# Issuing the weight loads of the output projection and the FFN from GpSimd

## The chip, the cores and the metric

The kernel runs on one core of a Trainium2 chip. The metric is device time in microseconds for one execution; the time before is the median of three runs, and a profile of one execution is read beside it.

## The reference

One transformer block on 2,048 tokens of width 1,024, in float32. The core of it:

```python
h = rms_norm(x, g_attn) * (1 + sc_a) + sh_a
aq, ak, av, bq, bk, bv, iq, ik, iw = split(h @ w_in)
o_a = diff_attention(aq, ak, av)           # 4 heads, dense, difference of two softmaxes
o_b = dsa_attention(bq, bk, bv, iq, ik, iw)  # 8 heads over the 256 keys that an indexer picks
x = x + gt_a * (concat(o_a, o_b) @ w_out)
h = rms_norm(x, g_ffn) * (1 + sc_f) + sh_f
u = causal_dwconv(h @ w_up)                # 3 taps along the tokens, 2 * 2816 columns
x = x + gt_f * ((silu(u_gate) * u_val) @ w_down)
```

## The kernel before

Each float32 factor of a product is held as two fp16 parts, high and low, and `acc3` (lines 399 to 404) adds three matmuls per block of 128: high by high, high by low, low by high. The kernel has two phases. In the first, about the first 600 us and parts of the next 150, the weights are split into their two parts and written to DRAM (`wo_s`, `wu_s`, `wd_s`), and the projections by `w_in` are made. The second phase takes the 16 blocks of 128 tokens in six runs, `RUNS = [(0, 2), (2, 2), (4, 4), (8, 4), (12, 2), (14, 2)]` (first block, number of blocks). Each run has its selection (I), its dense attention (A), its sparse attention (B, C) and its output projection and FFN (F).

`ffn` (line 1257) does F. `out_proj` multiplies the mixed heads by `w_out` (16 tiles `wo` for four blocks, 8 for two). Then, for each of two halves of the hidden width, come 22 chunks of `w_up` of 128 columns (tiles `wu`, a gate chunk and a value chunk by turns), the convolution and the gate, and then the product by `w_down` (tiles `wd`, two output halves of six tiles each for every two blocks). All three kinds of tile share one ring of three buffers of 512 KB, 4 KB in each partition (`tag="wu"`, `BUFS["wu"]` is 3; the sixth `wd` of a half is 256 KB). So a load can start when the matmuls that read the third tile before it are done, and there are 64 + 264 + 192 = 520 such loads.

The convolution of a chunk is spread over three engines. ScalarE copies the product out of PSUM to `ut` (line 1274) and makes the third tap `ua` (line 1276), VectorE adds the second tap (line 1277), and GpSimd makes the first tap `u0` (line 1279), adds it (line 1280), and moves the two last columns from and to `halo` (lines 1273 and 1281). GpSimd also multiplies value by gate, once per two chunks (line 1287). Its work for the attention is small: a power for a norm (line 992), the mask added to a bias (line 1152) and the power of the second norm (line 1241).

The order of the work comes from generators that yield their cost: `timeline` (line 1314) always advances the part that is due next, so that F of a run goes beside the attention of the next one (`fpos`, `FK`). The F of the last run, blocks 14 and 15, has no attention left beside it. A scheduler then fixes each engine's program, in order, by its own clock; every engine and every issuing queue works through its list without overtaking. All transfers are issued by SyncE (SP below): the 520 weight loads, 480 DMA transposes of the attention weights (`pT`, line 922), and the keys, values, queries, masks and rows of x.

```python
wu = Z.tile([P, 2, KD, P], F16, name="wu", tag="wu", bufs=BUFS["wu"])
nc.sync.dma_start(wu, wu_s[cc // 4][:, cc % 4])
ps = mm_ps(w=n)
acc3(ps, lambda hl, k: wu[:, hl, k], lambda hl, k: hT[:, hl, k, :n], KD)
```

Of the kernel before, what the change touches and what calls it, by code (L numbers as in the profile page):

```python
# [13 lines left out]
F16 = mybir.dt.float16  # L14
# [6 lines left out]
DRAM = bass.MemoryType.DRAM  # L21

P = 128
# [17 lines left out]
# natural groups of columns of w_in: (name, [(first column, width)], kept width)  # L41
# [10 lines left out]
# share of the next run that a run's FFN is spread over  # L52
FK = [1, 1, 1, 1.2, 1.2, 1]
# from where to where in the second phase: first projections, others, selection, dense part, sparse part of two blocks
E0 = dict(M=(0, .1), N=(.1, 1), I=(0, .5), A=(0, .4), B=(.4, .7), C=(.7, 1))
# work of the preparation of the weights
RESTN = 4 + 13 * 9 + 37 + 11 * 5
SMALL = 6
SHORT = 8                # the block below which VectorE counts one block of two for all bits
ORDER = [4, 5, 3, 0, 1, 2]  # L60
NE = 4                   # tiles projected in the first phase
BUFS = dict(r2k=7, sq=2, wst=4, k4=4, big=4, ring=10, nb=5, q=4, qi=2, ki=2, hl=3, pT=4, f2k=8, g=12, wu=3, mask=2)
ATT0 = dict(big=6, ring=4, nb=5, q=4, ki=1, hl=3, pT=3)
# rates of that preparation, beside the projections and beside the first tiles
R_REST = 0.75
R_FIRST = 0.4
# runs of blocks of 128 tokens that the attention and the FFN take together
RUNS = [(0, 2), (2, 2), (4, 4), (8, 4), (12, 2), (14, 2)]
# from where to where among the runs their selection is made
# [3 lines left out]
def bucket_starts():  # L73
    """First distance of each of the buckets 17..31."""
    n = np.arange(1, 512, dtype=np.float32)
    large = 16 + (np.log(n / np.float32(16)) / np.float32(math.log(8.0)) * np.float32(16)).astype(np.int32)
    large = np.minimum(large, 31)
    return [int(n[np.argmax((large >= b) & (n >= 16))]) for b in range(17, 32)]
# [3 lines left out]
def block_kernel(ctx: ExitStack, tc, x, c, w_ada, b_ada, g_attn, w_in, q_norm_a, k_norm_a, q_norm_b, k_norm_b,  # L82
# [16 lines left out]
    # ---------------------------------------------------------------- constants  # L99
# [13 lines left out]
    def pow2_floor(out_, in_):  # L113
        """out_ = the largest power of two not above in_ > 0."""
        V.tensor_scalar(out_.bitcast(I32), in_.bitcast(I32), EXPM, None, op0=ALU.bitwise_and)

    def pow2_inv(out_, in_, e):
        """out_ = 2^e / in_ for in_ a power of two."""
        V.tensor_scalar(out_.bitcast(I32), in_.bitcast(I32), -1.0, float((254 + e) << 23), op0=ALU.mult, op1=ALU.add)

    def all_max(pool, out_, in_):
        """out_ = the largest magnitude of the column in_, in all partitions."""
# [6 lines left out]
    def woven(*gens):  # L129
        """The generators in step, each (generator, its work) at its own rate."""  # L130
# [20 lines left out]
    def pipeline(units):  # L151
        """Each unit is a list of generators, its stages; a stage runs in step with the next stage of the unit before."""
# [22 lines left out]
    # rows of 128 features to columns  # L175
# [35 lines left out]
    # ---------------------------------------------------------------- modulation  # L211
# [6 lines left out]
    def set_anchor(bi):  # L218
        """Work that is held is issued behind the newest anchor of its engine."""
# [8 lines left out]
    def pace(bi):  # L228
        """While pacing, side work keeps its place among the main work."""
# [19 lines left out]
    def ada(pool, g):  # L249
        """A part of the modulation, summed on VectorE: as columns, or (2, 5) as a row in all partitions."""  # L250
# [29 lines left out]
    def h_scale(pool, name, gT, g0):  # L280
        """Columns of the gain and shift of h, times a power of two that keeps |h|_2 < 2^14, and that power."""
# [18 lines left out]
    # ---------------------------------------------------------------- weights  # L300
    def w_load(pool, src):
        """The rows of 128 x nk of src, in two tiles."""
# [7 lines left out]
    def scale_of(mx, s, inv):  # L310
        """s = the power of two that brings the root of mx under 2^15, inv = 1 / s."""
# [7 lines left out]
    def prep(pool, tiles, dst, w, inv, s_out=None, n2_out=None, done=None, held=False, gain=None):  # L319
        """dst(i, 0 / 1) = the fp16 high and low parts of tiles[i] (times the row gain) * s, s a power of two that keeps  # L320
        the norm of every column (n2_out: the largest, squared), or else of all of it, under 2^15; inv gets 1 / s."""
# [54 lines left out]
    # ---------------------------------------------------------------- h = norm(x) * g + s, transposed, in two parts  # L376
    def rms_rows(xt, n, xn, junk):
        """xn = the n rows of 1024 of xt, normalised."""
# [8 lines left out]
    def h_chunk(pool, xn, k, gp, sp, hT, c0, tag, bufs):  # L387
        """hT[:, 0 / 1, k, c0...] from the normalised rows, 128 each."""
# [10 lines left out]
    def acc3(ps, a, b, nk, k0=0, first=True, last=True):  # L399
        """ps = sum over k of (a0 + a1)[k]^T (b0 + b1)[k] without the product of the low parts."""  # L400
# [5 lines left out]
    def split(hi, lo, src, scale):  # L406
        """hi + lo = src * scale."""
# [3 lines left out]
    # ---------------------------------------------------------------- scalars of the attention parts  # L411
    VS = 2.0 ** -14          # products of h and w_in to fp16
    QS = 2.0 ** 12           # normalised queries to fp16
    PB = 14                  # weights of the sparse part to fp16: times 2^PB
# [3 lines left out]
    def gain(pool, name, qg, kg):  # L418
        """Column of q gain * k gain / 8 (twice), times 2^m below 2^12, and 2^-(12 + m)."""
# [17 lines left out]
    # ---------------------------------------------------------------- projections  # L437
    ka_s = [dram.tile([P, 4, 4, 256], F16, name=f"ka_s{t}") for t in range(NT)]    # head, block, k of 2
    va_s = [dram.tile([P, 4, 4, 256], F16, name=f"va_s{t}") for t in range(NT)]    # head, block, v in 2 parts
    kb_s = [dram.tile([P, 2, 4, 256], F16, name=f"kb_s{t}") for t in range(NT)]    # group, block, k in 2 parts  # L440
    vb_s = [dram.tile([P, 2, 4, 128], F16, name=f"vb_s{t}") for t in range(NT)]    # group, block, v in 2 parts
# [20 lines left out]
    def w_in_first(pool, g, wg, tiles):  # L462
        """Parts of a group of w_in to SBUF and to DRAM."""
# [1016 lines left out]
```

## Time and profile before

| what | value |
|---|---|
| time, median of 3 runs (range) | 3296.61 us (3294.74 to 3297.13) |
| span of the profiled execution | 3288.9 us |
| TensorE matmuls (PE), share of the span | 86% |
| VectorE (DVE) | 78% |
| ScalarE (ACT) | 61% |
| GpSimd (POOL) | 37% |
| mean granted TensorE clock | 0.951 of full |
| mean DMA rate | 214 GB/s |

The profiled execution has no time of its own beside its span, which runs from its first to its last instruction; the runs' median is 7.7 us longer. In the profile PE stands for matmuls, PEld for weight loads into TensorE, and SPq for SyncE's queue, which issues transfers and does nothing else. An instruction that issues a transfer from SP is not counted as busy time.

### The profile page before, as it was taken

The page shows a single profiled execution, that of the slowest core. Times are in us where ns is not written, and L with a number is a line of the kernel's source. Part 1 is how long each engine was busy: PE and PEld are TensorE (multiplying, and loading weights), DVE is VectorE, ACT ScalarE, POOL GpSimd, SP SyncE. Part 2 cuts the span into 40 slices and gives each one's busy share as a digit, 9 for nine tenths or more (in the row PEclk, how much of TensorE's full clock was granted, in tenths as well). Part 3 has the DMA queues.
Part 4 walks back from the last instruction along what each step waited for, and adds up shares of the span by engine and source line. Part 5 has one row for each costly group of instructions (what it writes and reads, how often), then busy time and mean ns, then how long its engine had stood idle before and what let it go on. Part 6 is the DMA issues. An engine that isn't in the chain of part 4 may idle for free.

```text
span 3288.9 us, 54138 instructions
## 1 busy us (share of the span) xinstructions
PE 2831.8 (86%) x17571; PEld 1621.2 (49%) x17571; DVE 2573.9 (78%) x6915; ACT 2008.5 (61%) x3773; POOL 1214.3 (37%) x1493
## 2 busy tenths in 40 slices
PE   5879997986889889877998999789889898788899
PEld 2334544442756566533444444444444445556466
DVE  8856889886988999977998788796788977967222
ACT  3757755573755775777456975568746678556122
POOL 2100354220645255501750571006325502835155
PEclk9889998998999899988999999999999999999999
DMA  8699975427687778996458779974786697799776
GB/s 339 184 322 307 357 274 172 148 65 226 189 229 229 203 216 207 254 247 165 123 133 241 184 181 247 268 199 117 207 214 156 156 278 210 192 261 229 215 218 199
DMA packets 747268, 704.07 MB, mean 214 GB/s; under 512 B 480494, under 2 KB 589286, under 8 KB 745704
## 3 DMA queue, kind: packets, MB, share of 16 engines
q1 hardware_dynamic: 746984, 700.62, 76.2%
q8 instruction: 137, 2.24, 0.3%
q14 instruction: 147, 1.20, 0.1%
HBM read 480.88 MB, written 114.20 MB: 181 GB/s over the span
## 4 chain that ended last, share of the span: by engine, by line
PE 32%; DVE 29%; DMA 15%; ACT 10%; issue 10%; POOL 3%; SPq 1%; DVEq 0%; ACTq 0%; POOLq 0%
PE mm L402 8%; PE mm L403 8%; PE mm L404 8%; DMA pT<-hl 7%; ACT cjunk L1081 4%; DVE cjunk L1065 4%; DVE hl L409 3%; DMA wd<-wd_s 3%; DMA xt<-in_x_dram 2%; DVE sc L1043 2%; DMA wu<-wu_s 1%; DVE big L906 1%; DVE ua L1277 1%; DVE big L903 1%; DVE big L973 1%
## 5 line engine op out<-in xcount | busy, mean ns | idle before, releaser
L402 PE MATMUL mm<-h2T,wu 128*128 128x256 f16 (+1 forms) x2112 | 655.9, 311 | 33.8 <-ACT ua L1276 17.4
L404 PE MATMUL mm<-h2T,wu 128*128 128x256 f16 (+1 forms) x2112 | 656.3, 311 | 0.0
L403 PE MATMUL mm<-h2T,wu 128*128 128x256 f16 (+1 forms) x2112 | 655.8, 311 | 0.0
L1081 ACT ACTIVATE cjunk<-sc,sel 128x512 bf16<-128x512 f32 (+10 forms) x281 | 395.8, 1409 | 155.9 <-DVE cjunk L1065 118.7
L1279 POOL TENSOR_SCALAR u<-ut,cws 128x256 f32<-128x256 f32 (+1 forms) x264 | 343.3, 1301 | 343.1 <-ACT ut L1274 295.9
L402 PE MATMUL mm<-wd,gT 128*128 128x512 f16 x704 | 272.5, 387 | 52.8 <-DMA wd<-wd_s 34.8
L1280 POOL TENSOR_TENSOR ua<-ua,u 128x256 f32<-128x256 f32 (+1 forms) x264 | 279.9, 1061 | 60.4 <-DVE ua L1277 49.2
L403 PE MATMUL mm<-wd,gT 128*128 128x512 f16 x704 | 272.3, 387 | 0.0
L404 PE MATMUL mm<-wd,gT 128*128 128x512 f16 x704 | 271.8, 386 | 0.0
L402 PEld LDWEIGHTS <-wu 128*128 128x128 f16 x2112 | 208.8, 99 | 123.4 <-DMA wu<-wu_s 20.9
L403 PEld LDWEIGHTS <-wu 128*128 128x128 f16 x2112 | 208.4, 99 | 122.9 <-issue 25.6
L409 DVE SCALAR_TENSOR_TENSOR hl<-big,hl 128x512 f16<-128x512 f32 (+3 forms) x320 | 207.3, 663 | 72.5 <-ACT hl L408 71.7
L404 PEld LDWEIGHTS <-wu 128*128 128x128 f16 x2112 | 208.1, 99 | 103.6 <-issue 3.5
L408 ACT ACTIVATE hl<-big 128x512 f16<-128x512 f32 (+3 forms) x320 | 172.4, 562 | 140.0 <-DMA pT<-hl 135.4
L402 PE MATMUL mm<-wg,hT 128*128 128x512 f16 (+1 forms) x640 | 243.5, 381 | 16.5 <-DVE kn L487 8.4
L403 PE MATMUL mm<-wg,hT 128*128 128x512 f16 (+1 forms) x640 | 242.9, 380 | 3.0 <-DVE wg L371 3.0
L1277 DVE SCALAR_TENSOR_TENSOR ua<-ut,cws,ua 128x256 f32<-128x256 f32 (+1 forms) x264 | 161.1, 610 | 104.4 <-ACT ua L1276 97.3
L404 PE MATMUL mm<-wg,hT 128*128 128x512 f16 (+1 forms) x640 | 235.3, 377 | 2.2 <-DVE hT L396 2.2
L1043 DVE SCALAR_TENSOR_TENSOR sc<-relu,iw_all,sc 128x512 f32<-128x512 f32 (+3 forms) x266 | 220.3, 828 | 17.7 <-ACT relu L1042 14.5
L481 POOL TENSOR_TENSOR hn_r<-hn_t,mhalf 128x8 f32<-128x8 f32 (+1 forms) x64 | 96.1, 1504 | 371.0 <-DVE hn_t L479 254.6
L992 POOL TENSOR_TENSOR a_ss<-a_ss,mhalf 128x1 f32<-128x1 f32 x64 | 44.2, 690 | 506.9 <-DVE a_ss L991 344.2
L1042 ACT ACTIVATE relu<-si 128x512 f32<-128x512 f32 (+3 forms) x266 | 139.8, 540 | 122.1 <-PE si L1035 75.4
(338 smaller groups left out, 7349.7 us busy)
## 6 DMA issues: line engine op xcount, KB each, us to landing
wu<-wu_s SPq DMA_DIRECT2D x264, 512.0 KB, 4.2
wd<-wd_s SPq DMA_DIRECT2D x160, 512.0 KB, 4.8
wo<-wo_s SPq DMA_DIRECT2D x64, 512.0 KB, 5.0
wst<-in_w_ada_dram SPq DMA_DIRECT2D x22, 1024.0 KB, 12.8
wst<-in_w_up_dram SPq DMA_DIRECT2D x22, 1024.0 KB, 10.5
wu_s<-wp SPq DMA_DIRECT2D x22, 1024.0 KB, 5.8
xd<-x_s SPq DMA_DIRECT2D x64, 256.0 KB, 5.0
ka<-ka_s SPq DMA_DIRECT2D x60, 256.0 KB, 4.6
```

Of the source, the lines that this page charges most:

```text
L402: PE.matmul(ps, a(0, k), b(0, k), start=(first and k == k0), stop=False)
L403: PE.matmul(ps, a(0, k), b(1, k), start=False, stop=False)
L404: PE.matmul(ps, a(1, k), b(0, k), start=False, stop=(last and k == k0 + nk - 1))
L408: S.activation(hi, src, AF.Copy, scale=scale)
L409: V.scalar_tensor_tensor(lo, src, scale, hi, op0=ALU.mult, op1=ALU.subtract)
L1042: S.activation(r, ps, AF.Relu)
L1043: V.scalar_tensor_tensor(sc_[:, c0:c1], r, w, sc_[:, c0:c1], op0=ALU.mult, op1=ALU.add)
L1065: V.tensor_scalar(junk[:, :ns[j]], src[j][:, :ns[j]], C[:, j:j + 1].bitcast(F32), None, op0=op, op1=ALU.add, accum_out=cnt[:, j:j + 1])
L1081: S.activation(junk[:, :ns[j]], scs[j][:, :ns[j]], AF.Sign, bias=C[:, j:j + 1].bitcast(F32), accum_out=cnt[:, j:j + 1])
L1277: V.scalar_tensor_tensor(a, ut[:, 1:n + 1], cws[:, 1, cc:cc + 1], a, op0=ALU.mult, op1=ALU.add)
L1279: G.tensor_scalar(u0, ut[:, 0:n], cws[:, 0, cc:cc + 1], None, op0=ALU.mult)
L1280: G.tensor_tensor(a, a, u0, op=ALU.add)
```

## The change

The three kinds of weight load of the second phase are issued by GpSimd and no longer by SyncE; everything else stays. (The rest of the difference removes comments.)

```diff
@@ out_proj
                     wo = Z.tile([P, 2, 2, 512], F16, name="wo", tag="wu", bufs=BUFS["wu"])
-                    nc.sync.dma_start(wo, wo_s[:, half, k0:k0 + 2])
+                    nc.gpsimd.dma_start(wo, wo_s[:, half, k0:k0 + 2])
@@ ffn
                     wu = Z.tile([P, 2, KD, P], F16, name="wu", tag="wu", bufs=BUFS["wu"])
-                    nc.sync.dma_start(wu, wu_s[cc // 4][:, cc % 4])
+                    nc.gpsimd.dma_start(wu, wu_s[cc // 4][:, cc % 4])
@@ ffn
                         wd = Z.tile([P, 2, 2, 512], F16, name="wd", tag="wu", bufs=BUFS["wu"])
-                        nc.sync.dma_start(wd[:, :k1 - k0], wd_s[half][:, 11 * hf_ + k0:11 * hf_ + k1])
+                        nc.gpsimd.dma_start(wd[:, :k1 - k0], wd_s[half][:, 11 * hf_ + k0:11 * hf_ + k1])
```

The scheduler makes new programs for all engines from this. First, GpSimd's program late in the chunks of `w_up` of the last run, for one pair of chunks (gate and value; the numbers count tiles in the order of the source, names in brackets are semaphores waited for). Before:

```order
L1279 TENSOR_SCALAR u0_36775<-ut_36769,cws_169 128x256 [waits Activation_49]
L1281 COPY halo_174<-ut_36769 128x2
L1273 COPY ut_36806<-halo_174 128x2
L1280 TENSOR_TENSOR ua_36772<-ua_36772,u0_36775 128x256 [waits DVE_49,Pool_49]
L1279 TENSOR_SCALAR u0_36812<-ut_36806,cws_169 128x256 [waits Activation_49,Pool_49]
L1281 COPY halo_174<-ut_36806 128x2
L1273 COPY ut_36850<-halo_174 128x2 [waits DVE_49]
L1280 TENSOR_TENSOR ua_36809<-ua_36809,u0_36812 128x256 [waits DVE_49,Pool_49]
L1287 TENSOR_TENSOR ua_36772<-ua_36772,ua_36809 128x256 [waits DVE_49,Pool_49]
```

The same stretch after the change:

```order
L1269 DMA wu_36698<-wu_s9_153 128x2048 [waits DMASW4_49,PE_49]
L1280 TENSOR_TENSOR ua_36529<-ua_36529,u0_36532 128x256 [waits DVE_49,Pool_49]
L1279 TENSOR_SCALAR u0_36569<-ut_36563,cws_169 128x256 [waits Activation_49,Pool_49]
L1281 COPY halo_174<-ut_36563 128x2
L1269 DMA wu_36742<-wu_s4_148 128x2048 [waits DMASW5_49,PE_49]
L1273 COPY ut_36607<-halo_174 128x2 [waits Pool_49]
L1280 TENSOR_TENSOR ua_36566<-ua_36566,u0_36569 128x256 [waits DVE_49,Pool_49]
L1279 TENSOR_SCALAR u0_36613<-ut_36607,cws_169 128x256 [waits Activation_49,Pool_49]
L1281 COPY halo_174<-ut_36607 128x2
L1273 COPY ut_36644<-halo_174 128x2 [waits DVE_49]
L1287 TENSOR_TENSOR ua_36529<-ua_36529,ua_36566 128x256 [waits Pool_49]
```

The pair keeps its nine operations and gets two loads among them. A load waits for TensorE to be done with the third tile before its own, and the additions of older chunks stand behind it.

Second, GpSimd's program early in the second phase, around the power of one head's norm in the dense attention (`a_ss_11709`, line 992). Before, it stands behind the operations of a chunk of `w_up`:

```order
L1279 TENSOR_SCALAR u0_11231<-ut_11225,cws_169 128x256 [waits Activation_49,Pool_49]
L1281 COPY halo_174<-ut_11225 128x2
L1280 TENSOR_TENSOR ua_11228<-ua_11228,u0_11231 128x256 [waits DVE_49,Pool_49]
L1287 TENSOR_TENSOR ua_11162<-ua_11162,ua_11228 128x256 [waits DVE_49,Pool_49]
L992 TENSOR_TENSOR a_ss_11709<-a_ss_11709,mhalf_70 128x1 [waits DVE_49]
```

After the change:

```order
L1302 DMA wd_9828<-wd_s1_156 128x2048 [waits DMASW4_49,PE_49]
L1302 DMA wd_9855<-wd_s1_156 128x2048 [waits DMASW5_49,PE_49]
L1302 DMA wd_9901<-wd_s1_156 128x1024 [waits DMASW6_49,PE_49]
L1269 DMA wu_9913<-wu_s2_146 128x2048 [waits DMASW7_49,PE_49]
L1269 DMA wu_9979<-wu_s8_152 128x2048 [waits DMASW0_49,PE_49]
L1269 DMA wu_10042<-wu_s3_147 128x2048 [waits DMASW1_49,PE_49]
L992 TENSOR_TENSOR a_ss_11709<-a_ss_11709,mhalf_70 128x1 [waits DVE_49]
L1269 DMA wu_10110<-wu_s8_152 128x2048 [waits DMASW2_49,PE_49]
```

The same power now stands behind loads, each of which waits for TensorE, and beside earlier chunks of the FFN than before (those with numbers near 9,900, where it was 11,225): the scheduler has set the FFN of the first runs later against the attention.

## Rows read from the trace of the kernel before

**Rows 1.** The page: busy time by engine, and the chain that ended last.

```profile
PE 2831.8 (86%) x17571; PEld 1621.2 (49%) x17571; DVE 2573.9 (78%) x6915; ACT 2008.5 (61%) x3773; POOL 1214.3 (37%) x1493
...
PE 32%; DVE 29%; DMA 15%; ACT 10%; issue 10%; POOL 3%; SPq 1%; DVEq 0%; ACTq 0%; POOLq 0%
PE mm L402 8%; PE mm L403 8%; PE mm L404 8%; DMA pT<-hl 7%; ACT cjunk L1081 4%; DVE cjunk L1065 4%; DVE hl L409 3%; DMA wd<-wd_s 3%; DMA xt<-in_x_dram 2%; DVE sc L1043 2%; DMA wu<-wu_s 1%; DVE big L906 1%; DVE ua L1277 1%; DVE big L903 1%; DVE big L973 1%
```

**Rows 2.** Busy time by stretch: from:to and length, PE, PEld, DVE, ACT, POOL, clock, DMA.

```profile
833.00:909.00 76.00, 68.08 (x609) 57.44 (x609) 71.94 (x250) 56.69 (x146) 56.99 (x103) 1.00 0.73 204
952.00:1028.00 76.00, 71.19 (x623) 58.80 (x624) 67.27 (x145) 43.84 (x106) 62.85 (x91) 1.00 0.73 209
1125.00:1207.00 82.00, 76.90 (x671) 63.14 (x670) 78.86 (x264) 63.90 (x148) 58.13 (x97) 0.99 0.72 200
1252.00:1360.00 108.00, 97.44 (x869) 74.47 (x867) 104.43 (x297) 76.94 (x193) 76.79 (x112) 0.98 0.92 222
1808.00:1960.00 152.00, 147.78 (x937) 75.43 (x935) 122.98 (x338) 133.87 (x229) 96.24 (x106) 0.99 0.80 182
...
3104.00:3162.00 58.00, 58.00 (x524) 51.62 (x524) 19.65 (x46) 26.02 (x63) 48.48 (x92) 0.98 0.60 184
3195.00:3254.00 59.00, 57.95 (x527) 51.22 (x527) 19.00 (x43) 25.57 (x62) 48.87 (x94) 1.00 0.69 208
```

**Rows 3.** Timeline of POOL, one pair of chunks of the last run: start, us, operation.

```profile
3116.13 0.92 POOL L1279 TENSOR_SCALAR u<-ut,cws 128x256 f32<-128x256 f32 x1 [0.41 <-ACT ut L1274]
3117.00 0.37 POOL L1281 COPY halo<-ut 128x2 f32<-128x2 f32 x1
3117.31 0.18 POOL L1273 COPY ut<-halo 128x2 f32<-128x2 f32 x1
3117.45 0.72 POOL L1280 TENSOR_TENSOR ua<-ua,u 128x256 f32<-128x256 f32 x1
3118.26 0.72 POOL L1287 TENSOR_TENSOR ua<-ua 128x256 f32<-128x256 f32 x1
3118.96 0.92 POOL L1279 TENSOR_SCALAR u<-ut,cws 128x256 f32<-128x256 f32 x1
3119.83 0.32 POOL L1281 COPY halo<-ut 128x2 f32<-128x2 f32 x1
3120.09 0.18 POOL L1273 COPY ut<-halo 128x2 f32<-128x2 f32 x1
3120.23 0.72 POOL L1280 TENSOR_TENSOR ua<-ua,u 128x256 f32<-128x256 f32 x1
3121.37 0.93 POOL L1279 TENSOR_SCALAR u<-ut,cws 128x256 f32<-128x256 f32 x1 [0.42 <-ACT ut L1274]
```

**Rows 4.** Two issuing lines of SP: ns shortest/median/longest, first and last start.

```profile
L1269 SPq DMA_DIRECT2D wu<-wu_s x264: 319/324/1482, 807.8 to 3246.5; - x132
...
L922 SPq DMA_TRANSPOSE pT<-hl x480: 1167/1239/4354, 592.2 to 3045.3; - x160
```

**Rows 5.** Who waited for whom: us in total, times, longest.

```profile
POOL a_ss L992 <- DVE a_ss L991: 344.2, 34, 73.1
...
PE mm L402 <- DMA wd<-wd_s: 34.8, 31, 6.2
...
PE mm L402 <- DMA wo<-wo_s: 30.3, 15, 10.4
...
PE mm L402 <- DMA wu<-wu_s: 14.3, 12, 2.9
```

**Rows 6.** The same for SP's queue, the two longest on weight loads.

```profile
SPq L1269 <- PE mm L404: 301.5, 115, 12.3
...
SPq L1302 <- PE mm L404: 154.8, 82, 9.0
```

**Rows 7.** Loads of the last run, 3100 to 3289 us: count, KB, median us to landing.

```profile
wu<-wu_s SPq DMA_DIRECT2D x41, 512.0 KB, 4.1
wd<-wd_s SPq DMA_DIRECT2D x20, 512.0 KB, 4.0
```

## The prediction

> **What bounds the kernel now.** I read the page first. TensorE is busy 86% and VectorE 78% of the span, and the chain that ended last changes between TensorE (32%), VectorE (29%) and transfers (15%) [rows 1]: no one engine sets the time throughout. GpSimd (POOL) is busy 37% [rows 1], which looks like room for 520 more instructions. That mean is misleading, so I read the busy times by stretch next. Each stretch shown is one half of an FFN's 22 chunks of `w_up`. In the four early ones (runs of two blocks, with attention beside them) POOL is busy 57.0 of 76, 62.9 of 76, 58.1 of 82 and 76.8 of 108 us; beside the attention of a longer run, with four blocks in the FFN, 96.2 of 152 us [rows 2]. In the last run, where no attention is left, it is busy 48.5 of 58 and 48.9 of 59 us while TensorE is busy without a gap, 58.0 of 58 [rows 2]. So TensorE bounds that stretch and POOL is close behind it.
>
> The timeline of POOL there shows how close. A pair of chunks takes 3121.37 - 3116.13 = 5.24 us, the time of 48 matmuls, and POOL waits in it once, 0.42 us [rows 3]. Its own work is 4.82 us a pair, 92% of it. Eleven such pairs make a half, so 22 pairs stand in the tail. That is where I look for the cost; SP's queue is where I look for the gain.
>
> **The change part by part.** It takes 520 issues from SP and gives POOL the same 520. The bytes and the three buffers stay. The pieces of the order show that the change does this, and where the new instructions stand.
>
> *What an issue costs POOL* is the number on which all rests, and the trace has none: POOL issues nothing before. From below the nearest row is POOL's shortest operation, the copy of two columns, 0.18 us [rows 3]; from above SP's issue of a transpose, 1.24 us median, where a plain issue holds SP 0.32 us [rows 4]. I take 1.0 us. A load of 512 KB is 128 rows of 4 KB, read on one side and written on the other, so 256 entries of a list; POOL's operation on 256 elements per partition takes 0.92 us [rows 3] and the longer of SP's two issues 1.24 us, and I put the list between those. This is a choice, and both ends stay for the range. The Trainium skill (DMA: Bandwidth & Descriptors, "Anatomy of one DMA — SWDGE (gpsimd) path") speaks against it: it calls descriptor generation small and says most of a transfer's fixed cost is its completion, off the engine. By that page the first term below would shrink towards 0; no run here shows it yet.
>
> *The tail's 44 chunks.* A pair on POOL becomes 4.82 + 2 x 1.0 = 6.82 us against TensorE's 5.24, so POOL takes over as the bound: 22 x (6.82 - 5.24) = +34.8 us. With 0.18 us the pair is 5.18, still under 5.24: 0. With 1.24 it is 7.30: +45.3 us. The cover that hid POOL's work was TensorE's matmuls, and 0.42 us a pair is all that was left of it.
>
> *The early stretches of two blocks.* With 22 us each, POOL's demand is 79.0 of 76, 84.9 of 76, 80.1 of 82 and 98.8 of 108 us. The excess is 3.0 + 8.9 = 11.9 us if POOL never waited; at 98% and more it will wait, so I take +15. Some of this comes back, since VectorE is at 71.9 of 76 and 104.4 of 108 us there [rows 2] and attention can use what the FFN leaves. Ends: 0 (0.18 us) and 8.3 + 14.2 + 3.4 = +25.9 (1.24 us). In the runs of four blocks 96.2 + 22 = 118.2 of 152 us fits: 0.
>
> *What queues behind a load on POOL.* A load waits on POOL for TensorE, and what stands behind waits too. The convolution's operations need TensorE's later chunks anyway, so for them it is nearly free. The attention's powers are not tied to the FFN; in the second piece of the order one stands behind three `wd` and three `wu` loads, each released by the end of one tile, 5.24 / 2 = 2.62 us. VectorE waits for that power. Before, POOL mostly stood ready for it: 344.2 us in 34 waits [rows 5], so the power had no slack on POOL's side. I take +8 us for all 64 powers and the mask additions. Ends: 0, and +40 (in each of the 10 `w_down` parts beside attention about 1.5 tiles of 2.62 us).
>
> *Landing.* In the tail a load lands 4.1 (`wu`) or 4.0 us (`wd`) after its issue [rows 7], and with three buffers a tile's round is 2.62 + 4.0 us, a third of which is 2.21. An issue of 1.0 in place of 0.32 us makes it 2.43, still under 2.62: 0, at most +3.
>
> *What SP gains.* Its queue loses 520 x 0.32 = 168 us of issuing, and the waits for TensorE at the head of its queue, 301.5 + 154.8 us for `wu` and `wd` [rows 6], during which nothing behind could start. Little of it lies on the path: SP's queue is 1% of the chain [rows 1], and transposes hold SP 1.24 us each with or without loads between them. What it can give is bounded by TensorE's waits for loads, 34.8 + 30.3 + 14.3 = 79.4 us [rows 5]; about half of these are loads that stood behind other transfers in SP's queue, so -40 at best. But POOL will now make loads late too. I take -10; ends -40 and 0.
>
> *Sum:* 34.8 + 15 + 8 + 0 - 10 = +47.8 us. The profiled execution spans 3288.9 us, the median is 3296.6; I add the change to the median: 3344.4 us, say **3344 us**. All low ends together give 3257, all high ends 3297 + 45 + 26 + 40 + 3 = 3411.
>
> **The rivals.** *Faster: a light issue.* If an issue holds POOL no more than (5.24 - 4.82) / 2 = 0.21 us, TensorE stays the bound of the tail, and what is left is SP's relief: transposes no longer stand behind loads that wait for a buffer, and loads no longer behind transposes. `pT` is 7% of the chain [rows 1], and TensorE's waits for loads are 79.4 us. I give it -30: 3267 us. For it: SP's plain issue is 0.32 us, not far off. Against it: POOL's shortest operation of all is 0.18 us, and a list for 128 rows is more work than copying two columns.
>
> *No change.* An issue somewhere near 0.4 us costs the tail 22 x (5.62 - 5.24) = 8.4 us, the early stretches next to nothing (62.9 + 8.8 of 76), and the gain at SP pays it back: 3297 us. The Trainium skill (DMA: Bandwidth & Descriptors, "Issuing engines are not separate DMA queues") says about this: which engine issues only saves that engine's time, usually small beside the transfer, as all transfers share the same DMA engines. By that rule the time stays within a few us of 3297; the 1% of SP's queue in the chain agrees with its half about SP, and it does not count what else the new issuer has to do.
>
> *Much slower: loads held behind attention.* POOL's list is in order, so a load behind a power waits until VectorE has that power's operand. POOL stood 34 times for this, 10.1 us a time and up to 73.1 us [rows 5]; nothing hung on it. TensorE has two tiles in hand, 5.24 us. Where a wait outlasts those, TensorE stops, and with it the attention's own matmuls in its list. If all 34 waits kept loads behind them, 34 x (10.1 - 5.24) = 165 us; with half of them about 80 us come on top of my sum: 3425 us. For it: the second piece of the order has a load right behind a power. Against it: the scheduler places loads and powers by its clock, and early ones are set apart.
>
> **How the numbers follow.** My case has a chance of 0.64, with 3303 to 3400 as its own range; the light issue 0.14, no change 0.10, loads behind attention 0.12. A measurement can tell 0.2%, 6.6 us, from no change, so from 3290 to 3303 is "same". Faster: 0.14 and a little of "no change", 0.16. Same: most of the rest of that case and the lowest end of mine, 0.08. Slower: 0.76. The range 3284 to 3412 leaves out most of the light issue (0.12) and two thirds of the last rival (0.08); its top is the sum of the high ends.
>
> **What would show it.** In the new profile the 41 loads of `w_up` that fall into the tail should stand among POOL's operations with about 1.0 us each; a pair there should take about 6.8 us where it took 5.24, POOL should have no idle time in it, and TensorE should wait 1.6 us a pair, its busy time in a half near 58 of 75 us. The stretch of the tail should grow by about 35 of the 48 us. The `w_down` parts of the tail should keep their length, and SP's queue should show its transposes starting earlier. I am wrong about the mechanism if the tail keeps its length, and about its size if an issue takes under 0.5 us or the early runs change by more than the tail. TensorE's waits for `wd` and `wo` beyond 79 us in all, or long waits of loads behind powers, would speak for the last rival.

## The result, and the profile after

The changed kernel takes 3465.32 us (median of 4 runs, 3458.48 to 3469.54), the kernel before 3295.68 us beside it (4 runs, 3287.26 to 3297.13). The ratio is 1.0521, 95% interval 1.0497 to 1.0545: 170 us slower, where 48 were forecast. The direction is right; the size lies 53 us above the top of the range. Where single profiles are compared below, the changed kernel's spans 3467.8 us.

The page of the changed kernel, its busy times, queues and chain (compare [rows 1]):

```profile
PE 2901.6 (84%) x17571; PEld 1643.7 (47%) x17571; DVE 2651.3 (76%) x6915; ACT 2015.1 (58%) x3773; POOL 1477.0 (43%) x2013
...
q1 hardware_dynamic: 672104, 436.35, 48.8%
q0 software_dynamic: 72832, 264.27, 25.5%
...
PE 30%; DVE 27%; DMA 20%; issue 10%; ACT 8%; POOL 4%; SPq 1%; DVEq 0%; ACTq 0%; POOLq 0%
DMA pT<-hl 13%; PE mm L402 7%; PE mm L403 7%; PE mm L404 7%; ACT cjunk L1081 3%; DVE cjunk L1065 3%; DVE hl L409 3%; DMA wd<-wd_s 2%; DMA xt<-in_x_dram 2%; DVE big L906 1%; DVE ua L1277 1%; DVE big L903 1%; POOL ua L1280 1%; DMA wo<-wo_s 1%; DVE big L908 1%
```

The 264 MB of the loads now go through a queue of their own (q0). What grew in the chain is the transposes `pT`, from 7% of 3289 us to 13% of 3468, about 220 us more; no other entry shown grew by more than a point. Those transposes were not moved.

Busy times by stretch, the same columns as in [rows 2]: the four halves of early runs, then the two halves of the last run.

```profile
834.00:950.00 116.00, 86.89 (x701) 68.08 (x698) 105.54 (x364) 79.64 (x203) 76.47 (x133) 0.88 0.69 172
997.00:1077.00 80.00, 77.11 (x624) 60.87 (x623) 73.97 (x130) 46.81 (x106) 71.65 (x115) 0.99 0.64 185
1177.00:1273.00 96.00, 81.07 (x679) 65.37 (x679) 94.39 (x266) 60.66 (x143) 79.50 (x122) 0.95 0.67 172
1323.00:1417.00 94.00, 84.16 (x777) 67.61 (x777) 85.88 (x245) 62.69 (x150) 70.90 (x123) 0.98 0.91 217
3258.00:3324.00 66.00, 61.21 (x528) 52.28 (x528) 35.44 (x45) 25.07 (x63) 57.91 (x107) 0.97 0.54 162
3361.50:3427.50 66.00, 59.71 (x528) 51.15 (x529) 33.67 (x40) 24.23 (x61) 58.26 (x108) 1.00 0.60 186
```

A half of the tail takes 66 us where it took 59. The early halves hold other shares of attention than before (364 VectorE operations in the first, where there were 250), so their lengths can't be compared one by one. Therefore I compare three points in time: the first matmul of the third run's output projection, that of the last run's, and the last matmul of all. In the profiled executions these are 1414.4, 3067.9 and 3285.2 us before and 1474.2, 3224.3 and 3464.1 after. So the 179 us between the two profiles fall into three parts:

| part | growth |
|---|---|
| early: up to the third run's output projection | +59.8 us |
| middle: from there to the last run's | +96.5 us |
| tail: the last run's output projection and FFN, no attention beside it | +22.6 us |

Not all of the growth is waiting. TensorE's matmuls, the same 17571, are busy 2901.6 us where it was 2831.8 (the page above and [rows 1]), at a mean granted clock of 0.933 where it was 0.951. Of these 70 us, 37 lie in the middle part and 8 in the tail. The runs below whose middle grows by 90 us or more show it too (granted clock 0.940 in e4, 0.937 in e9, 0.934 in e7, 0.939 in e14). No run separates the lower clock from the waits, so a loss below is both together.

A pair of chunks on POOL in the tail (compare [rows 3]):

```profile
3289.86 1.10 POOL L1279 TENSOR_SCALAR u<-ut,cws 128x256 f32<-128x256 f32 x1
3290.92 0.17 POOL L1281 COPY halo<-ut 128x2 f32<-128x2 f32 x1
3291.04 0.17 POOL L1273 COPY ut<-halo 128x2 f32<-128x2 f32 x1
3291.18 0.71 POOL L1287 TENSOR_TENSOR ua<-ua 128x256 f32<-128x256 f32 x1
3291.85 0.59 POOL L1269 DMA_DIRECT2D wu<-wu_s  x1
3292.46 0.77 POOL L1280 TENSOR_TENSOR ua<-ua,u 128x256 f32<-128x256 f32 x1
3293.23 1.08 POOL L1279 TENSOR_SCALAR u<-ut,cws 128x256 f32<-128x256 f32 x1
3294.27 0.17 POOL L1281 COPY halo<-ut 128x2 f32<-128x2 f32 x1
3294.39 0.59 POOL L1269 DMA_DIRECT2D wu<-wu_s  x1
3294.99 0.20 POOL L1273 COPY ut<-halo 128x2 f32<-128x2 f32 x1
3295.13 0.73 POOL L1280 TENSOR_TENSOR ua<-ua,u 128x256 f32<-128x256 f32 x1
3295.83 1.11 POOL L1279 TENSOR_SCALAR u<-ut,cws 128x256 f32<-128x256 f32 x1
```

POOL has no idle time in it, and the pair takes 3295.83 - 3289.86 = 5.97 us; eleven of them are the 66 us of a half. The issue takes 0.59 us, not 1.0. Over all 264 chunks, and the waits for weights (compare [rows 4, 5]):

```profile
L1269 POOL DMA_DIRECT2D wu<-wu_s x264: 527/595/992, 799.1 to 3419.3; - x132
```

```profile
POOL wd L1302 <- PE mm L404: 335.3, 116, 12.8
...
POOL wo L1222 <- PE mm L404: 194.3, 45, 22.2
POOL wu L1269 <- PE mm L404: 181.4, 69, 13.5
POOL a_ss L992 <- DVE a_ss L991: 107.9, 31, 9.3
```

```profile
PE mm L402 <- DMA wd<-wd_s: 25.0, 17, 4.8
...
PE mm L402 <- DMA wo<-wo_s: 18.7, 14, 6.1
...
PE mm L402 <- DMA wu<-wu_s: 10.2, 15, 1.8
```

Loads now stand 711 us at the head of POOL's list, and still TensorE waits less for weights than before: 53.9 us where it was 79.4. What it waits for is the transposes. First the kernel before, who waited for `pT` and its time from issue to landing, then the changed one:

```profile
  ACT hl L408: 158.9, 109
...
  PE o L1176: 47.9, 42
  PE o L981: 38.4, 27
...
DMA to landing us min/median/max: 2.3/3.5/7.1
```

```profile
  ACT hl L408: 212.1, 107
...
  PE o L1176: 112.0, 67
...
  PE o L981: 73.6, 40
...
DMA to landing us min/median/max: 2.4/4.9/10.9
```

A transpose lands 1.4 us later by the median, and TensorE's matmuls wait for it 112.0 + 73.6 = 186 us, before 86. Of the 99 us more, 69 fall into the middle part (142 us, 72 before) and 30 into the early one. ScalarE, whose `hl` is free only then, waits 212 where it was 159. The transpose is not issued later: paired with the end of the operation that makes its `hl`, its median delay on SP fell from 0.52 to 0.22 us (the mean stays near 1.0).

### The profile page after: what moved, and what is told of

Same layout as the page of the kernel before. It is cut to its first block, busy times and chain, and to the rows that moved or that the text cites. A ratio compares the mean times of both kernels' runs of the same rounds, so it can differ in the third digit from the quotient of the medians.

```text
span 3467.8 us, 54228 instructions
## 1 busy us (share of the span) xinstructions
PE 2901.6 (84%) x17571; PEld 1643.7 (47%) x17571; DVE 2651.3 (76%) x6915; ACT 2015.1 (58%) x3773; POOL 1477.0 (43%) x2013
## 3 DMA queue, kind: packets, MB, share of 16 engines
q0 software_dynamic: 72832, 264.27, 25.5%
## 4 chain that ended last, share of the span: by engine, by line
PE 30%; DVE 27%; DMA 20%; issue 10%; ACT 8%; POOL 4%; SPq 1%; DVEq 0%; ACTq 0%; POOLq 0%
DMA pT<-hl 13%; PE mm L402 7%; PE mm L403 7%; PE mm L404 7%; ACT cjunk L1081 3%; DVE cjunk L1065 3%; DVE hl L409 3%; DMA wd<-wd_s 2%; DMA xt<-in_x_dram 2%; DVE big L906 1%; DVE ua L1277 1%; DVE big L903 1%; POOL ua L1280 1%; DMA wo<-wo_s 1%; DVE big L908 1%
## 5 line engine op out<-in xcount | busy, mean ns | idle before, releaser
L402 PE MATMUL mm<-h2T,wu 128*128 128x256 f16 (+1 forms) x2112 | 665.3, 316 | 43.7 <-ACT ua L1276 29.9
L403 PE MATMUL mm<-h2T,wu 128*128 128x256 f16 (+1 forms) x2112 | 665.0, 315 | 0.0
L404 PE MATMUL mm<-h2T,wu 128*128 128x256 f16 (+1 forms) x2112 | 664.0, 315 | 0.0
L1279 POOL TENSOR_SCALAR u<-ut,cws 128x256 f32<-128x256 f32 (+1 forms) x264 | 350.4, 1327 | 108.8 <-ACT ut L1274 100.6
L409 DVE SCALAR_TENSOR_TENSOR hl<-big,hl 128x512 f16<-128x512 f32 (+3 forms) x320 | 218.5, 697 | 114.6 <-ACT hl L408 114.0
L402 PE MATMUL mm<-wd,gT 128*128 128x512 f16 x704 | 279.0, 396 | 31.0 <-DMA wd<-wd_s 25.0
L1280 POOL TENSOR_TENSOR ua<-ua,u 128x256 f32<-128x256 f32 (+1 forms) x264 | 264.6, 1002 | 57.7 <-DVE ua L1277 43.5
L403 PEld LDWEIGHTS <-wu 128*128 128x128 f16 x2112 | 211.5, 100 | 144.0 <-issue 43.1
L403 PE MATMUL mm<-wd,gT 128*128 128x512 f16 x704 | 278.9, 396 | 0.0
L404 PE MATMUL mm<-wd,gT 128*128 128x512 f16 x704 | 278.0, 395 | 0.0
L1277 DVE SCALAR_TENSOR_TENSOR ua<-ut,cws,ua 128x256 f32<-128x256 f32 (+1 forms) x264 | 199.6, 756 | 100.3 <-ACT ua L1276 56.4
L1302 POOL DMA_DIRECT2D wd<-wd_s x192 | 108.1, 563 | 386.3 <-PE mm L404 335.3
L402 PEld LDWEIGHTS <-wu 128*128 128x128 f16 x2112 | 212.4, 101 | 124.1 <-DMA wu<-wu_s 17.6
L404 PEld LDWEIGHTS <-wu 128*128 128x128 f16 x2112 | 211.6, 100 | 105.2 <-issue 2.8
L402 PE MATMUL mm<-wg,hT 128*128 128x512 f16 (+1 forms) x640 | 244.3, 382 | 16.6 <-DVE kn L487 8.2
L1269 POOL DMA_DIRECT2D wu<-wu_s x264 | 155.4, 589 | 238.4 <-PE mm L404 181.4
L403 PE MATMUL mm<-wg,hT 128*128 128x512 f16 (+1 forms) x640 | 243.4, 381 | 2.9 <-DVE wg L371 2.9
L1176 PE MATMUL o<-vb,pT 128*128 128x128 f16 x1088 | 137.9, 227 | 126.9 <-DMA pT<-hl 112.0
```

What stands on the lines that cost most here:

```text
L402: PE.matmul(ps, a(0, k), b(0, k), start=(first and k == k0), stop=False)
L403: PE.matmul(ps, a(0, k), b(1, k), start=False, stop=False)
L404: PE.matmul(ps, a(1, k), b(0, k), start=False, stop=(last and k == k0 + nk - 1))
L409: V.scalar_tensor_tensor(lo, src, scale, hi, op0=ALU.mult, op1=ALU.subtract)
L1176: PE.matmul(po[:, 0:128], hi, v[:, 0:128], start=(j == 0), stop=False)
L1269: nc.gpsimd.dma_start(wu, wu_s[cc // 4][:, cc % 4])
```

## The experiments

**The theory**, as it stood in the end (up to e6 it had one cause for all outside the tail). In the middle, loads on a second queue run beside the transposes on the same DMA engines and make them late, whoever issues them. Early and in the tail, the time that GpSimd's issues take out of its in-order list costs. **Rivals:** GpSimd's issues cost everywhere (1); the scheduler, which lays out all programs anew, made a worse order (2); the bytes hurt in another way than through the transposes (3).

The parts in the table are worked out as above, each from one profile against its base. Executions of one kernel differ by 10 us and more (3287.26 to 3297.13 for the kernel before), so smaller parts mean nothing.

| run | loads issued by | ratio to before (95%) | early | middle | tail |
|---|---|---|---|---|---|
| changed kernel | GpSimd | 1.0521 (1.0497 to 1.0545) | +60 | +97 | +23 |
| e1 | GpSimd in the last run alone | 1.0073 (1.0046 to 1.0099) | -3 | +12 | +23 |
| e2, quarter loads | SyncE | 0.9901 (0.9883 to 0.9920) | base of e3 | | |
| e3, quarter loads | GpSimd | 0.9957 (0.9940 to 0.9974) | +12 | -12 | +14 |
| e4 | ScalarE | 1.0397 (1.0376 to 1.0418) | +10 | +116 | -2 |
| e5, no transposes | SyncE | 0.9643 (0.9616 to 0.9670) | base of e6 | | |
| e6, no transposes | GpSimd | 0.9957 (0.9935 to 0.9980) | +63 | +10 | +22 |
| e7, order for 0.57 us | GpSimd | 1.0549 (1.0514 to 1.0584) | +52 | +106 | +14 |
| e8, other order | SyncE | 0.9990 (0.9976 to 1.0004) | +3 | -1 | +1 |
| e9 | SyncE in two runs, then GpSimd | 1.0466 (1.0428 to 1.0504) | -1 | +147 | +22 |
| e10 | GpSimd in two runs, then SyncE | 1.0220 (1.0173 to 1.0267) | +72 | 0 | -1 |
| e11, split loads | both | 1.0251 (1.0217 to 1.0286) | +51 | +26 | +11 |
| e12, longer lag | SyncE | 0.9999 (0.9984 to 1.0014) | -6 | +5 | +2 |
| e13 | as e10, order of before | 1.0175 (1.0149 to 1.0200) | +59 | +7 | +2 |
| e14 | GpSimd, order of before | 1.0509 (1.0477 to 1.0541) | +35 | +94 | +28 |
| e15, idle issues | SyncE | 1.0158 (1.0126 to 1.0191) | +30 | +27 | -3 |

### The tail alone

```diff
-nc.gpsimd.dma_start(wu, ...)
+(nc.gpsimd if b0 == 14 else nc.sync).dma_start(wu, ...)
```

> Only the loads of the last run of blocks (where no attention is left) are issued by GpSimd; all earlier ones stay with SyncE. Between the two kernels the tail grew by 23 us of the 170 us. Theory (the loads on a second queue run beside the attention's transposes and make them land later): there are no transposes in the tail, so only the tail's own cost is left, +20 to +25 us, near 3318 us. Rival 1 (each issue and the wait at its head cost GpSimd time wherever the FFN runs): the tail has 104 of the 520 loads, so 104/520 x 170 = +34 us, near 3330 us. Either way the tail's halves of w_up should take 65 to 66 us as in the changed kernel, against 58 to 59 before; a tail that keeps its 58 us would mean that its growth came in from earlier work.

3317.39 against 3293.55 us, +24 us: the halves of `w_up` take 65.3 and 64.3 us. This is the tail's own cost, as the theory has it; rival 1's +34 lies above it.

### Quarter loads, on SyncE and on GpSimd

```diff
-nc.sync.dma_start(wu, wu_s[cc // 4][:, cc % 4])
+nc.sync.dma_start(wu[:, 0, 0:4], wu_s[cc // 4][:, cc % 4, 0, 0:4])
-acc3(ps, lambda hl, k: wu[:, hl, k], ...)
+acc3(ps, lambda hl, k: wu[:, 0, k % 4], ...)
```

(`wo` and `wd` in the same way; e3 has `nc.gpsimd` in place of `nc.sync`.)

> Each load moves a quarter of its bytes (1 KB per partition; the matmuls use that quarter again, so the weights of the products are left out for the most part), all loads issued by SyncE, number and place of all instructions as before. It is the base for the next run. The theory and its rivals alike expect it no slower than the kernel before: 3200 to 3300 us. If the DMA engines' time matters to the transposes even on one queue, their median from issue to landing falls under 3.5 us.

> The same quarter loads (most of the weights left out of the products), issued by GpSimd. Theory (bytes of the loads beside the transposes on the shared DMA engines make these late): with a quarter of the bytes the transposes land nearly as early as with all loads on SyncE, and the difference to the run of quarter loads on SyncE shrinks from 170 us to about 30 to 70 us, the tail's 23 among it. Rivals 1 and 2 (the issue's time on GpSimd, or the order that the scheduler sets for it) do not depend on bytes: the difference stays at 140 to 170 us, with transposes landing as in the changed kernel, 4.9 us median, or not.

3259.22 and 3279.51 us: the difference is 20 us, and 14 of them are in the tail. GpSimd's 520 issues are as long as with full loads (for `wu` 0.590 us median, 0.595 there), and they wait for TensorE nearly as long (604 us at the head of GpSimd's list, 711 there). With a quarter of the bytes the transposes land after 3.4 us (3.2 in e2), and 150 of the 170 us are gone. So the issues by themselves do not cost 170 us, and the bytes matter. It falls below what the theory gave (30 to 70), since here the early part is nearly gone too (+12), which the theory did not say and no later run explains. The scheduler lays out another order for smaller loads, so this pair alone did not exclude rival 2.

### The loads on ScalarE

```diff
-nc.gpsimd.dma_start(wu, ...)
+nc.scalar.dma_start(wu, ...)
```

> All three kinds of loads are issued by ScalarE, GpSimd gets none. Theory (a second queue beside the transposes): the transposes' median from issue to landing rises to 4.5 us or more as with GpSimd, TensorE waits for them by over 150 us in sum (before 86), and the time is 3380 us or more. Rival 1 (GpSimd's issue): GpSimd is free of the loads, transposes land at 3.5 us, GpSimd's tail pairs are back at 5.24 us, and any loss is ScalarE's own: loads waiting at the head of its list and holding its copies behind them.

3423.31 us, +130 us without a load on GpSimd. The trace shows the same picture at the transposes: who waits for `pT`, and its landing.

```profile
  ACT hl L408: 225.7, 106
...
  PE o L981: 87.6, 41
  PE o L1176: 73.2, 47
...
DMA to landing us min/median/max: 2.4/4.7/12.4
```

TensorE's matmuls wait 160.8 us, the middle grows by 116, and the tail, in which there are no transposes, does not grow at all. So a loss in the middle comes with either second queue, and the tail's with GpSimd alone. One rival of this run stays: the loads also stand at the head of ScalarE's list, some 122 us in the middle, and hold up its own work. Early they stand there some 65 us and 10 us are lost; how much of the middle's 116 is ScalarE's own was not separated.

### Without the transposes

```diff
-pp = X.tile([P, 8, P], F16, name="pT", bufs=BUFS["pT"])
-nc.sync.dma_start(pp[:, :2 * (b1 - b0)], hl[:, :2 * w], transpose=True)
+pp = hl.rearrange("p (n q) -> p n q", q=P)
```

(`hl` also gets the buffers of `pT`; e6 is the same with `nc.gpsimd` for the loads.)

> The 480 DMA transposes are left out: attention multiplies with its weights as they stand in hl, untransposed, so its products are not those of the reference; every matmul and every other transfer stays, hl has the buffers of pT. All loads with SyncE. It is the base for the next run. All theories: faster than the kernel before, 3050 to 3250 us, since the waits of ScalarE and TensorE for pT (159 and 86 us) are gone.

> The same without the transposes, with the loads issued by GpSimd, at their full 512 KB. Theory (loads of a second queue make the transposes late, and that is where the time outside the tail went): with no transposes to delay, the difference to the run before this one is the tail's 23 us and little more, 20 to 50 us. Rivals: if the loads' bytes hurt through other transfers of SyncE, or through their own later landing, or if GpSimd's issue or the scheduler's order cost it, 120 to 170 us of difference stay.

3174.29 and 3280.29 us. The difference is 106 us, not 20 to 50: the theory of one cause outside the tail fell here. The parts show what stands and what doesn't. The middle's loss is down to 10 us, so it does go through the transposes, and rival 3 is out for it. The early part keeps its 63 us: that has another cause. From here on the early part is a question of its own.

### Other orders

```diff
+_spec.SWDGE_FIXED_OVERHEAD_NS = 480        # e7, all loads on GpSimd
+_spec.HWDGE_FIXED_OVERHEAD_NS = {..., SP: 700}    # e8, all loads on SyncE (shortened)
```

> The changed kernel, but the scheduler's estimate for an issue on GpSimd is cut to about the 0.57 us measured, so that it lays out another order for all engines (loads still on GpSimd). Theory: transposes land as late as in the changed kernel (4.9 us median) and the time stays at 3430 to 3490 us whatever the order. Rival 2 (the order laid out for a dear issue is what costs): 100 us or more come back, 3300 to 3370 us.

> The kernel before (all loads with SyncE), but the scheduler's estimate for an issue on SyncE is raised by an eighth, which makes it lay out another order for all engines. It measures what another order alone is worth. Theory: the order is worth some tens of us at most, 3270 to 3330 us, and the transposes land at 3.5 us. Rival 2: orders differ by 100 us or more, so this one may be as slow as the changed kernel.

3472.38 and 3293.00 us. A new order on SyncE is worth nothing (0.9990; its transposes land after 3.8 us, 3.5 before), and the changed kernel in a new order is as slow, with transposes landing after 5.1 us. Rival 2 is out for the loss as a whole.

### Early and late runs apart

```diff
-nc.gpsimd.dma_start(wu, ...)
+(nc.sync if b0 < 4 else nc.gpsimd).dma_start(wu, ...)    # e9; e10 the reverse
```

> Loads with SyncE in the first two runs of blocks, with GpSimd in the later four. So far the traces split the 170 us of the changed kernel in three: about 60 us up to the output projection of the third run (there also without transposes, 63 us), about 90 us beside the long attention rows behind it (gone without transposes), 23 us in the tail. Theory (three separate causes, in their own places): only the first part is undone, +115 us, 3400 to 3425 us. Rival (the early delay pushes FFN work under later attention, and that is what costs there): with the early part undone most of the later loss goes too, 3300 to 3350 us.

> The reverse: GpSimd issues the loads of the first two runs of blocks alone, SyncE the others. Theory (separate causes): +50 to +65 us, 3345 to 3360 us, and none of it is given back later. Rival (the early stretch only changes the order in which attention and FFN are done): the loss is given back behind it, 3295 to 3315 us.

3447.78 us, +154, and 3368.23 us, +74. Both are above their expectation, e9 most clearly (its time was put at 3425 at most). The losses are separate in place, and nothing of the early one is given back, but they do not add: 74 + 154 = 228 us, together they cost 170. With the early part undone the middle loses 147 us, not 97. Why it loses less behind a late start stays open.

### The issues without the bytes

```diff
-nc.gpsimd.dma_start(wu, src)
+nc.sync.dma_start(f(wu)[:, :1920], f(src)[:, :1920])
+nc.gpsimd.dma_start(f(wu)[:, 1920:], f(src)[:, 1920:])
```

(`src` stands for the tile in DRAM, `f` lays a partition's row of 2048 values out flat; `wo` and `wd` in the same way.)

> Every load is cut in two: SyncE moves all but the last 256 bytes of each partition's row, GpSimd those 256 bytes. GpSimd has all 520 issues with their waits, and nearly no bytes; nothing is left out. Theory (transposes are made late by the bytes that a second queue brings beside them): they land at 3.5 to 3.8 us again, TensorE waits for them about 90 us in sum, and the loss of the middle part is gone; what GpSimd's issues cost by themselves is left, early and in the tail: 3315 us if as little as with quarter loads, 3375 us if all of the early loss is theirs. Rival 1 (it is issues on GpSimd, not bytes, that cost everywhere): 3430 to 3470 us.

3375.85 us, +82. The landing of the transposes, e3 first and then e11:

```profile
DMA to landing us min/median/max: 2.3/3.4/5.6
```

```profile
DMA to landing us min/median/max: 2.3/3.8/9.4
```

TensorE's matmuls wait 94.2 us for them, as the theory has it, and the middle grows by 26 instead of 97. The time is the upper of the two values, but in part by luck: the tail grew by 11 and not by 23, and the 26 us of the middle were expected to be gone. The transposes are no reason for them (77 us of waits there, 72 before); what costs there stays open. The early loss, +51, needs nearly no bytes on GpSimd's queue. This kernel issues 1040 loads, 520 on SyncE as before.

### Another lag

```diff
-    LAG = 2
+    LAG = 3
```

> The kernel before (all loads with SyncE), but attention takes up the products of a transposed piece three pieces later instead of two. If the flight of the transposes is what attention waits for, covering more of it gives time even with loads on SyncE: 3270 to 3290 us. If the waits sit at the last piece of each row, which this does not move, nothing changes: 3290 to 3300 us.

3293.40 against 3293.78 us: no difference. Taking up a piece one step later covers nothing; it moves only the first pieces of a row, so this agrees with waits at a row's last piece and is no proof of them.

### What of GpSimd costs early

```diff
+_spec.SWDGE_FIXED_OVERHEAD_NS = 0          # e13 (issuers as in e10), e14, e15
+_spec.SWDGE_NS_PER_DESCRIPTOR = 0.0
```

```diff
                     hc = G.tensor_copy(halo[:, cc], ut[:, n:n + 2])
+                    if b0 < 4:                                   # e15, loads on SyncE
+                        for e in range(2):
+                            nc.gpsimd.dma_start(dmy[b0 // 2, cc, e], cws[:, 0, 0:16])
+                            ...                              # ordered behind hc
```

> As the run with GpSimd's loads in the first two runs of blocks alone, but the scheduler's estimate of an issue on GpSimd is set to nothing, so that it lays out nearly the order of the kernel before (in VectorE's list, 24 attention units of the sparse part stand before the 44th chunk, 27 in the kernel before, 32 with the dear issue). If the issues themselves are what costs (GpSimd's time, VectorE slowed, loads late in its list), the loss stays: 3340 to 3370 us. If the other order is what costs: 3295 to 3315 us.

> The changed kernel with all loads on GpSimd and nearly the order of the kernel before, by the same estimate. Theory (transposes late, about 90 us; tail 23 us; early loss by the issues themselves, 50 to 60 us): 3440 to 3480 us. If the early loss is the order's: 3400 to 3420 us. If the order is what costs everywhere: 3320 us or less.

> All loads with SyncE in nearly the order of the kernel before. In the first two runs of blocks GpSimd issues two stores of 64 bytes per partition behind each chunk's convolution, 176 in all, of data that nobody waits for, to a place that nobody reads. They cost GpSimd 176 x 0.57 = 100 us, as the 152 loads there cost it 87 us. If the early loss is the time of the issues on GpSimd and what they do to VectorE: 3335 to 3365 us, with VectorE's operations longer by 20 us or more in sum. If it is that loads come late out of GpSimd's list: 3290 to 3310 us.

3350.14 us (+54), 3461.02 us (+165) and 3346.17 us (+50). With nearly the order of before the loss stays; e14's early part, +35 where the changed kernel has +60, leaves room for some share of the order. And 176 issues that nobody waits for cost 50 us, although every load is back on SyncE. So issues cost by themselves, without a late load. By the parts 30 of the 50 us are early, where the issues are. The other 27 lie in the middle, where GpSimd issues nothing and TensorE waits 62 us for transposes, 72 before; they are not explained. Nor is it explained why the 152 issues of the same two runs cost only 12 us early in e3.

Who waited for the convolution's tile `ua` between 777 us and the third run's output projection; first the kernel before, then e15, whose added lines shift the numbers:

```profile
  ACT gT L408: 25.6, 16
...
  PE mm L402: 6.0, 7
...
  ACT uth L1285: 4.8, 7
```

```profile
  ACT gT L408: 67.9, 31
  PE mm L402: 25.7, 18
  ACT uth L1292: 21.5, 21
```

GpSimd's two last operations of a chunk come later, ScalarE waits for them at the head of its list, and the copies and third taps that free TensorE's accumulators stand behind: TensorE's wait for them grows from 6.0 to 25.7 us.

VectorE works longer, too. Busy times from 777 us to that output projection, the kernel before and e15, in the columns of [rows 2]:

```profile
777.00:1414.00 637.00, 560.37 (x4083) 376.09 (x4081) 568.15 (x1812) 408.75 (x951) 295.12 (x465) 0.96 0.83 226
777.00:1444.00 667.00, 563.34 (x4052) 377.14 (x4050) 586.97 (x1789) 407.09 (x947) 382.63 (x639) 0.96 0.80 215
```

Taken one by one, its operations are 22 us longer in sum than at their mean length before, as the expectation had it, and 11 of the 22 are the second tap. In the changed kernel's early part it is 21 us, and no run without GpSimd's issues in that part has more than 5.2. So the trace shows two ways in which the issues cost there: the waits on GpSimd's part of the chain, and a slower VectorE, which was busy 89% of that time. How much each costs was not separated.

## Why the prediction was right or wrong

- **What an issue costs POOL** (taken as 1.0 us, ends 0.18 and 1.24): 0.59 us in the tail, 0.60 median for `wu`. Inside the ends, but the choice by the length of the list was wrong: a load of the same 128 rows with a quarter of the bytes takes 0.590 us, and a store of 8 KB 0.581.
- **The tail's 44 chunks** (+34.8): the mechanism is as forecast, only the term's size was off. With the measured issue the working gives 4.82 + 2 x 0.59 = 6.00 us a pair, and the trace has 5.97; 22 x (5.97 - 5.24) = 16.1 us. The halves took 58.7 and 59.3 us from first to last matmul, and now 65.6 and 65.7: +13.3. That the `w_down` parts would keep their length was wrong: 32.3 and 31.0 us became 36.8 and 36.2, +9.6; TensorE's waits for `wd` in that stretch rose from 4.2 to 10.7 us, and the granted clock of those parts was 0.95 where it was 1.00. With what changed around the output projection that is the 23 us.
- **The early stretches** (+15, by POOL's excess over the stretch's length): this step failed. With 0.59 us an issue its working says 62.9 + 13.0 = 75.9 of 76 us at the worst, so next to nothing; the changed kernel lost 60 us there, and GpSimd's loads in the first two runs alone cost 54 and 74 (e13, e10). In e15 POOL was busy 57% of that time (382.63 of 667 us), and the issues still cost. POOL stands in the middle of a chain between other engines, and its lateness, with VectorE slowed beside it, cost long before it was full; the excess over the stretch's length was the wrong measure, and 98% was no threshold.
- **What queues behind a load on POOL** (+8): no sign of it. VectorE waited 9.1 us for POOL's powers in all, and POOL's own wait for their operands fell from 344.2 [rows 5] to 107.9 us. The rival of loads held behind powers would have shown as TensorE waiting for weights; that wait fell.
- **Landing** (0, at most +3): too low for `wd` in the tail, where the waits above grew by 6.5 us; a full `wd` lands there after 4.7 us by the median, 4.0 before [rows 7].
- **What SP gains** (-10, ends -40 and 0): the step that failed most. Both halves of its reasoning came true: transposes are issued sooner, and TensorE waits 25.5 us less for weights. But I looked at the queue as a place to wait in and not as what keeps transfers apart. With the loads on another queue the transposes land 1.4 us later, TensorE waits 99 us longer for them, 69 of it in the middle, and the middle, which I had at nothing, loses 97 us. In e3, e6 and e11 nearly all or most of that loss is gone: with a quarter of the bytes, without transposes, and with the bytes back on SyncE. The upper end of this term should not have been 0.
- **The rivals.** Light issue and no change did not come. Beside "no change" stood a rule of the Trainium skill (DMA: Bandwidth & Descriptors, "Issuing engines are not separate DMA queues"), that another issuing engine only saves issue time. The measurements differ: with ScalarE as issuer, where the tail does not grow, the kernel is 4.0% slower. A sentence of the same page fits better (section "Queues, rings and completion order"): each DMA engine takes the queues that have work in turn, a packet at a time. The landing times of e3, e4 and e11 agree with it; no run here shows single packets in turn.
- **What would show it.** "The early runs change by more than the tail" was named as what would make the size wrong, and it did. The direction is no proof of the account: its main term, the tail, is 23 of the 179 us between the profiles.

## What to carry to other kernels

Before moving large loads to another queue, look for small transfers with someone waiting for them that stay on the old one: one queue's order may be what keeps the loads out of their way, and a second queue gives that up, whichever engine issues it. An engine that computes in a chain and issues transfers too is costed by what its delay does to the next engine in the chain; the busy share of its stretch says little. And a term that looks like pure relief needs an end on the other side.

## What was not expected of the hardware

GpSimd's issue took nearly the same time whatever it moved: for `wu` the medians are 0.595 us with 512 KB, 0.590 with 128 KB and 0.588 with 32 KB, and a store of 8 KB took 0.581. The `wd` and `wo` loads of the changed kernel took 0.551 and 0.537.

Some VectorE operations take twice as long in the tail of the changed kernel, where GpSimd's pairs run without a gap. The groups of VectorE in the first half of `w_up` there, before and then after:

```profile
L1277 DVE SCALAR_TENSOR_TENSOR ua<-ut,cws,ua 128x256 f32<-128x256 f32 x21 | 11.1, 527 | 38.3 <-ACT ua L1276 36.7 <-POOL ua L1280 1.6
L409 DVE SCALAR_TENSOR_TENSOR gT<-ua,sgk,gT 128x256 f16<-128x256 f32 x10 | 4.7, 473 | 0.0
L1286 DVE SCALAR_TENSOR_TENSOR ua<-uth,ua 128x256 f32<-128x256 f32 x10 | 4.2, 419 | 0.0
```

```profile
L1277 DVE SCALAR_TENSOR_TENSOR ua<-ut,cws,ua 128x256 f32<-128x256 f32 x20 | 20.9, 1043 | 27.9 <-POOL ut L1273 19.1 <-ACT ua L1276 8.8
L409 DVE SCALAR_TENSOR_TENSOR gT<-ua,sgk,gT 128x256 f16<-128x256 f32 x9 | 9.0, 995 | 0.7 <-ACT gT L408 0.7
L1286 DVE SCALAR_TENSOR_TENSOR ua<-uth,ua 128x256 f32<-128x256 f32 x10 | 4.3, 427 | 1.9 <-ACT uth L1285 1.9
```

The Trainium skill (SBUF — State Buffer, "SBUF: two separate sides") says that a VectorE operation with two inputs from SBUF and a GpSimd operation that reads SBUF shut each other out for a whole instruction. The first two rows agree, the third, with two inputs as well, does not slow down. The traces show what they met. In the tail of the changed kernel 41 of the 44 second taps (L1277) ran beside one of GpSimd's operations with two inputs of 128x256 (L1280, L1287), and 39 of them took over 0.7 us; in the kernel before none of 44 met one; the third row's 22 met none. In e15's early part 31 second taps met such an operation, and 28 of them took over 0.7 us; 29 met an issue but no such operation, and 27 of those stayed under 0.7, the median 0.475. So what goes with the long operations is not the issue but GpSimd's two-input operations, which the fuller list brings beside VectorE's. The rule names any GpSimd operation that reads SBUF; the one-input L1279 ran beside all 44 second taps of the tail before, and they took 0.48 to 0.59 us. How much of the tail's 23 us this is stays open.
